# A mixture-of-experts decoder step on one core: scores of the next chunks between products, six outputs kept in PSUM, one bank each for scores and products

## The chip, the cores and the metric

One NeuronCore of a Trainium2 chip; the other cores are idle. The time is device microseconds of one execution of the whole program. TensorE is PE here, VectorE DVE, ScalarE ACT, GpSimd POOL, and SyncE, which issues most transfers, SP.

## The reference

One layer of a decoder trunk, for a prompt of 1024 tokens and for 8 sample sequences of one token each. The first half (normalisation, one projection, three mixers, output projection) is not touched by the change. The second half is PEER: each token picks, by two sets of 128 product keys, 16 experts in each of 8 heads out of 16,384, and each expert is one row of a table u and one row of a table v:

```
e_idx = i1 * N_KEYS + i2          # (n, 8 heads, 16) -> 128 experts per token
act = gelu(einsum('nd,nkd->nk', x, u_tab[e_idx]))
out = einsum('nk,nkd->nd', gate * act, v_tab[e_idx])
```

All in fp32; u_tab and v_tab hold 16,384 rows of 1024 numbers (4 KB a row, 64 MB a table).

## The kernel before

The 1024 prompt tokens are eight tiles of 128. Up to about 1720 us the kernel runs the first half and picks the experts. Then two ways of computing the experts run side by side.

**Gathered tiles** (prompt tiles 0, 2, 6 and 7, and the sample tile). For each of a token's 128 experts POOL issues an indirect transfer (L893, `gather_rows`) that brings one row of u per token, 128 rows of 4 KB, 512 KB in all, into one of five buffers `grow`; DVE multiplies and sums it (L901). After all 128, gelu and the gate, the same with v (L910, which adds into `acc`). L917 and L918 (`finish`) add the residual to a tile and SP stores it. The tiles come one after the other; the sample tile, eight rows of each table, is last, followed by a few small transfers and a reduction over its partial sums.

**Dense tiles** (prompt tiles 1, 3, 4 and 5, 512 tokens). Here all 16,384 experts are computed for all tokens, and a table of gates `g_d`, built before and zero where an expert wasn't picked, selects. There are 128 chunks of 128 experts. For each chunk `scores` loads 512 KB of u (L992), splits it into a high and a low part (`split`: cast on ACT, L968; difference on DVE, L969; named uh, ul), and multiplies by the tokens in 24 matmuls into one PSUM bank psS (L999: 8 pieces of the contraction, three products of high and low parts); ACT's gelu writes `a` (L1002), DVE multiplies by the gates gc (L1004; 2 MB of gates, for 8 chunks, are loaded by L989 into a single buffer), and `a` is split into ah and al. `load_v` loads 512 KB of v (L983) and splits it into vh, vl. Tables u and v come into RAW buffers `raw`, the split v into VB = 5.

Four chunks are a group. `products` multiplies a group's four `a` by its four v: eight outputs (4 tiles x 2 halves of 512 columns) of 12 matmuls each (L1015). RES of the outputs stay in PSUM over all groups (psK, the dictionary `keep`); the others go through the banks psO and are added by DVE to `acc` in SBUF (first group: copied, L1022; then L1024). PSUM has eight banks: four psK, two psS (SB) and two psO (OB). The loop runs one chunk ahead (SKEW = 1), so that PE works through the scores of four chunks and then through the eight products.

Both ways are written one after the other in the program; a scheduler that runs when the program is built puts each engine's instructions into one fixed order, by their dependences and estimated durations. So in the dense stretch each of DVE's and SP's lists alternates between the two. Each engine works through its list in order and waits where an operand isn't there. After the last group DVE multiplies the outputs by the gate g2 (L1043), adds the residual (L1044), and SP stores four tiles (L1045).

Of the kernel before, what the change touches and what calls it, by code (L numbers as in the profile page):

```python
# [16 lines left out]
ALU = mybir.AluOpType  # L17
# [10 lines left out]
GRP = 4  # L28
# [3 lines left out]
GST = 8  # L32
LK = 2
SJ = 4
RES = 4
RAW = 6
VB = 5
AB = 2
A4 = 3
SB = 2  # L40
OB = 2
SKEW = 1
GA = 3
GO = 1
GQ = 2
P = 128
# [13 lines left out]
def kernel(ctx: ExitStack, tc: tile.TileContext, I, O):  # L60
    nc = tc.nc
    V, A, G, T, S = nc.vector, nc.scalar, nc.gpsimd, nc.tensor, nc.sync
# [151 lines left out]
    def gate_row(which, t, alloc):  # L214

        m = alloc("grw")
        if t == NT:
            S.dma_start(m[:8], mods[which][0:8, :])
        else:
            S.dma_start(m, dram_ap(mods[which], 8 * D, [[0, P], [1, D]]))  # L220
        return m
# [10 lines left out]
    def product(st, t, xT, w):  # L232

        ps = st.ps("psz", "a")
        if t < NT:
            for c in range(8):
                T.matmul(ps, xT[:, c, :], w(c), start=(c == 0), stop=(c == 7))  # L237
            return ps
        for kk in range(2):
            for j in range(4):  # L240
                T.matmul(ps[32 * j:32 * j + 32, :], xT[:, 2 * j + kk, :], w(2 * j + kk), start=(kk == 0), stop=(kk == 1))
        part = st.a2("part")
        A.copy(part, ps)
        ps = st.ps("psz")
        T.matmul(ps[:8, :], sel[:, 0:8], part, start=True, stop=True)
        return ps
# [706 lines left out]
    def dense():  # L953
        n = ND * P
        parts = [(0, n)] if n <= 512 else [(0, n // 2), (n // 2, n)]
        outs = [(t, hf) for t in range(ND) for hf in range(2)]
        with tc.tile_pool(name="dn", bufs=2) as dn, tc.tile_pool(name="dps", bufs=1, space=PSUM) as dps:
            def ps_tile(name, bufs):
                return dps.tile([P, 512], F32, tag=name, name=name, bufs=bufs)

            def raw(name):
                return dn.tile([P, D], F32, tag="raw", name=name, bufs=RAW)

            def split(x, shape, key, bufs, eng):

                hi = dn.tile(shape, F32R, tag=key + "h", name=key + "h", bufs=bufs)
                lo = dn.tile(shape, F32R, tag=key + "l", name=key + "l", bufs=bufs)
                A.copy(hi, x)  # L968
                eng.tensor_tensor(lo, x, hi, op=ALU.subtract)  # L969
                return hi, lo  # L970

            xs_ = []
            for c in range(8):
                xr = raw("xr")[:, :n]
                S.dma_start(xr, xT_d[:, c, :])
                xs_.append(split(xr, [P, n], f"x{c}", 1, V))
            keep = {o: ps_tile(f"psK{o[0]}{o[1]}", 1) for o in outs[:RES]}
            acc = {o: dn.tile([P, 512], F32, name=f"acc{o[0]}{o[1]}", bufs=1) for o in outs[RES:]}
            gcs = {}

            def load_v(c):
                v = raw("v")
                S.dma_start(v, I["peer_v"][c * P:(c + 1) * P, :])  # L983
                return split(v, [P, D], "v", VB, V)

            def scores(c):
                if c % GST == 0:
                    gc = dn.tile([P, n // TB, GST, TB], F32, tag="gc", name="gc", bufs=1)
                    S.dma_start(gc, g_d[c // GST])  # L989
                    gcs[c // GST] = gc  # L990
                u = raw("u").rearrange("p (c k) -> p c k", c=8)
                S.dma_start(u, I["peer_uT"][c])  # L992
                us_ = split(u, [P, 8, P], "u", 2, V)
                a = dn.tile([P, n], F32, tag="a", name="a", bufs=AB)
                pss = [ps_tile("psS", SB) for _ in parts]
                for ps, (n0, n1) in zip(pss, parts):
                    for j in range(8):
                        for q, (x, y) in enumerate(((0, 0), (0, 1), (1, 0))):
                            T.matmul(ps[:, :n1 - n0], us_[x][:, j, :], xs_[j][y][:, n0:n1],  # L999
                                     start=(j == 0 and q == 0), stop=(j == 7 and q == 2))  # L1000
                for ps, (n0, n1) in zip(pss, parts):
                    A.activation(a[:, n0:n1], ps[:, :n1 - n0], AF.Gelu_apprx_tanh)  # L1002
                a3 = a.rearrange("p (b n) -> p b n", n=TB)
                V.tensor_tensor(a3, a3, gcs[c // GST][:, :, c % GST, :], op=ALU.mult)  # L1004
                return split(a, [P, n], "a", GRP + 1, V)

            def products(g, as_, vs_):
                first, last = g == 0, g == P // GRP - 1
                for o in outs:
                    t, hf = o  # L1010
                    ps = keep[o] if o in keep else ps_tile("psO", OB)
                    k = 0
                    for aa, vv in zip(as_, vs_):
                        for x, y in ((0, 0), (0, 1), (1, 0)):
                            T.matmul(ps, aa[x][:, t * P:(t + 1) * P], vv[y][:, hf * 512:(hf + 1) * 512],  # L1015
                                     start=(k == 0 and (first or o not in keep)),
                                     stop=(k == 3 * GRP - 1 and (last or o not in keep)))
                            k += 1
                    if o in keep:
                        continue  # L1020
                    if first:
                        V.tensor_copy(acc[o], ps)  # L1022
                    else:
                        V.tensor_tensor(acc[o], acc[o], ps, op=ALU.add)  # L1024

            ahead = [scores(c) for c in range(SKEW)]
            for g in range(P // GRP):
                as_ = list(ahead)
                vs_ = []
                for c in range(g * GRP, (g + 1) * GRP):  # L1030
                    if c >= g * GRP + SKEW:
                        as_.append(scores(c))
                    vs_.append(load_v(c))
                ahead = [scores(c) for c in range((g + 1) * GRP, (g + 1) * GRP + SKEW) if c < P]
                products(g, as_, vs_)
            g2 = gate_row("g2", DENSE[0], raw)
            for j, t in enumerate(DENSE):
                x1, tmp = raw("x1f"), raw("tmp")
                S.dma_start(x1, x1_d[t])
                for hf in range(2):  # L1040
                    sl = slice(hf * 512, (hf + 1) * 512)
                    src = keep[j, hf] if (j, hf) in keep else acc[j, hf]
                    V.tensor_tensor(tmp[:, sl], g2[:, sl], src, op=ALU.mult)  # L1043
                V.tensor_tensor(x1, x1, tmp, op=ALU.add)  # L1044
                S.dma_start(O["xp"][t * P:(t + 1) * P, :], x1)  # L1045
# [31 lines left out]
    for t in GROUPS[-1]:  # L1077
        if t in DENSE:
            now(select(t))
            now(gate_table(t))  # L1080
    fctx.close()
    dense()
    for t in GROUPS[-1]:
        if t not in DENSE:
# [91 lines left out]
```

## Time and profile before

| | us |
|---|---|
| median of 3 runs | 3323.45 (3322.58 to 3325.24) |
| profiled execution | 3327.76 |
| its span | 3326.0 |
| PE, DVE, ACT, POOL busy | 2795.2, 2543.4, 1201.9, 1394.1 |
| DMA | 952.56 MB, mean 286 GB/s |

The busy times are sums over stages with different limits. The change touches the last one alone, from about 1720 us to the end. A matmul's record shows 0.39 us or more, but the next starts earlier; how long a row of matmuls takes is read from the starts. The same holds on DVE and ACT, where a record reaches a little into the next.

### The profile page before, as it was taken

The page shows a single profiled execution, that of the slowest core. Times are in us where ns is not written, and L with a number is a line of the kernel's source. Part 1 is how long each engine was busy: PE and PEld are TensorE (multiplying, and loading weights), DVE is VectorE, ACT ScalarE, POOL GpSimd, SP SyncE. Part 2 cuts the span into 40 slices and gives each one's busy share as a digit, 9 for nine tenths or more (in the row PEclk, how much of TensorE's full clock was granted, in tenths as well). Part 3 has the DMA queues.
Part 4 walks back from the last instruction along what each step waited for, and adds up shares of the span by engine and source line. Part 5 has one row for each costly group of instructions (what it writes and reads, how often), then busy time and mean ns, then how long its engine had stood idle before and what let it go on. Part 6 is the DMA issues. An engine that isn't in the chain of part 4 may idle for free.

```text
span 3326.0 us, 35751 instructions
## 1 busy us (share of the span) xinstructions
PE 2795.2 (84%) x11152; PEld 1879.5 (57%) x11152; DVE 2543.4 (76%) x5342; ACT 1201.9 (36%) x2583; POOL 1394.1 (42%) x1046
## 2 busy tenths in 40 slices
PE   7999976868944888976759998988989988989997
PEld 2444353423630333554437777777777776777776
DVE  1324876896675777876799898788898888898896
ACT  2453474443630342664543222222222222222221
POOL 0000043414235532034323565466566656566563
PEclk8999997987955999987879999999999999999998
DMA  7556677947787987478887999899999999999996
GB/s 276 179 195 198 217 250 269 335 170 287 221 253 247 352 261 285 139 229 296 276 287 252 347 333 334 301 345 339 348 329 342 344 344 342 360 332 333 346 347 218
DMA packets 340157, 952.56 MB, mean 286 GB/s; under 512 B 35063, under 2 KB 117550, under 8 KB 337918
## 3 DMA queue, kind: packets, MB, share of 16 engines
q0 software_dynamic: 149760, 545.33, 46.6%
q1 hardware_dynamic: 190206, 404.95, 35.1%
q8 instruction: 88, 1.44, 0.2%
q14 instruction: 103, 0.84, 0.1%
HBM read 894.04 MB, written 60.85 MB: 287 GB/s over the span
## 4 chain that ended last, share of the span: by engine, by line
PE 27%; DMA 23%; issue 20%; POOL 14%; DVE 12%; ACT 3%; SPq 0%; POOLq 0%; DVEq 0%; ACTq 0%
POOL grow L893 14%; PE psz L237 10%; DMA grow<-in_peer_v,ge 8%; DMA g_d<-st 5%; PE psG L804 3%; DVE grow L901 3%; DMA grow<-in_peer_u,ge 2%; PE pst L162 2%; PE pso L622 2%; PE psS L999 2%; PE psO L1015 2%; PE lg L605 2%; PE psa L194 2%; DVE acc L910 1%; DMA w<-in_w_in 1%
## 5 line engine op out<-in xcount | busy, mean ns | idle before, releaser
L893 POOL DMA_INDIRECT grow<-in_peer_u,ge x520 | 685.2, 1318 | 1333.2 <-DVE grow L901 540.5
L893 POOL DMA_INDIRECT grow<-in_peer_v,ge x520 | 708.3, 1362 | 565.7 <-DVE acc L910 359.2
L910 DVE SCALAR_TENSOR_TENSOR acc<-grow,dot,acc 128x1024 f32<-128x1024 f32 x515 | 660.1, 1282 | 136.6 <-DMA grow<-in_peer_v,ge 129.5
L237 PE MATMUL psz<-w,hT 128*128 128x512 f32 x1408 | 682.7, 617 | 59.4 <-DMA w<-in_w_in 28.4
L901 DVE SCALAR_TENSOR_TENSOR grow<-grow,gx 128x1024 f32<-128x1024 f32 x520 | 625.8, 1219 | 133.5 <-DMA grow<-in_peer_u,ge 108.9
L237 PEld LDWEIGHTS psz<-w,hT 128*128 128x128 f32 x1408 | 253.2, 196 | 324.1 <-issue 223.0
L1015 PE MATMUL psO<-vh,ah 128*128 128x512 f32 x512 | 223.2, 436 | 120.8 <-DVE acc L1024 120.3
L804 PE MATMUL psG<-o,oh 128*128 128x128 f32 x1024 | 205.8, 339 | 121.0 <-ACT st L805 113.3
L968 ACT CAST vh<-v 128x1024 fp32r<-128x1024 f32 x128 | 125.2, 1048 | 492.5 <-PE psO L1015 491.1
L804 PEld LDWEIGHTS psG<-o,oh 128*128 128x128 f32 x1024 | 170.9, 232 | 208.7 <-ACT st L805 147.8
L796 DVE TENSOR_TENSOR oh<-iof,tr 128x1024 f32<-128x1024 f32 x128 | 156.5, 1224 | 134.2 <-PE psG L804 129.5
L968 ACT CAST ah<-a 128x512 fp32r<-128x512 f32 x128 | 79.6, 622 | 398.0 <-DVE a L1004 398.0
L968 ACT CAST uh<-u 128x1024 fp32r<-128x1024 f32 x128 | 135.1, 1055 | 236.6 <-PE psS L999 236.4
L1015 PE MATMUL psO<-vl,ah 128*128 128x512 f32 x512 | 216.9, 424 | 0.0
L1015 PE MATMUL psO<-vh,al 128*128 128x512 f32 x512 | 215.2, 420 | 0.0
L803 ACT ACTIVATE o<-oh,tr 128x128 f32<-128x128 f32 x512 | 185.5, 397 | 53.2 <-PE psG L804 44.0
L1015 PE MATMUL psK<-vh,al 128*128 128x512 f32 x512 | 199.9, 391 | 5.0 <-DVE al L969 5.0
L1015 PE MATMUL psK<-vh,ah 128*128 128x512 f32 x512 | 200.0, 391 | 2.3 <-ACT ah L968 2.3
L1015 PE MATMUL psK<-vl,ah 128*128 128x512 f32 x512 | 199.8, 390 | 0.0
L1015 PEld LDWEIGHTS psO<-vh,ah 128*128 128x128 f32 x512 | 107.2, 209 | 159.8 <-DVE acc L1024 136.3
L969 DVE TENSOR_TENSOR ul<-u,uh 128x1024 fp32r<-128x1024 f32 x128 | 156.1, 1220 | 5.5 <-ACT uh L968 5.5
L969 DVE TENSOR_TENSOR vl<-v,vh 128x1024 fp32r<-128x1024 f32 x128 | 150.6, 1219 | 0.5 <-ACT vh L968 0.4
(370 smaller groups left out, 5002.8 us busy)
## 6 DMA issues: line engine op xcount, KB each, us to landing
u<-in_peer_uT SPq DMA_DIRECT2D x128, 512.0 KB
v<-in_peer_v SPq DMA_DIRECT2D x128, 512.0 KB
w<-in_w_in SPq DMA_DIRECT2D x80, 512.0 KB
w<-in_wq SPq DMA_DIRECT2D x64, 512.0 KB
g_d<-st SPq DMA_DIRECT2D x32, 1024.0 KB
gc<-g_d SPq DMA_DIRECT2D x16, 2048.0 KB
w<-in_w_ada SPq DMA_DIRECT2D x48, 512.0 KB
w<-in_w_out SPq DMA_DIRECT2D x32, 512.0 KB
```

What stands on the lines that cost most here:

```text
L162: T.transpose(pv[:, c, :r], src[:, (c0 + c) * P:(c0 + c + 1) * P], ident[:r, :r])
L194: T.matmul(ps[32 * j:32 * j + 32, :], sc[:, 2 * j + kk, :], w(2 * j + kk), start=(kk == 0), stop=(kk == 1 and j > 0))
L237: T.matmul(ps, xT[:, c, :], w(c), start=(c == 0), stop=(c == 7))
L796: V.tensor_tensor(oh, iof[:, None, None, :].to_broadcast([P, 2, OHB, P]), tt[:, 0:2, b * TB + n0:b * TB + n0 + OHB, None].to_broadcast([P, ...
L803: A.activation(o1, oh[:, 0, n0 % OHB + q, :], AF.Copy, scale=tt[:, 2, n:n + 1])
L804: T.matmul(ps[:, q * P:(q + 1) * P], oh[:, 1, n0 % OHB + q, :], o1, start=True, stop=True)
L893: G.indirect_dma_start(out=rt, out_offset=None, in_=tab, in_offset=bass.IndirectOffsetOnAxis(ap=idx, axis=0))
L901: V.scalar_tensor_tensor(rt, rt, 1.0, x, op0=ALU.mult, op1=ALU.mult, accum_out=w[:, k:k + 1])
L910: V.scalar_tensor_tensor(acc, rt, w[:, k:k + 1], acc, op0=ALU.mult, op1=ALU.add)
L968: A.copy(hi, x)
L969: eng.tensor_tensor(lo, x, hi, op=ALU.subtract)
L1015: T.matmul(ps, aa[x][:, t * P:(t + 1) * P], vv[y][:, hf * 512:(hf + 1) * 512], start=(k == 0 and (first or o not in keep)), stop=(k == 3 * ...
```

## The change

- RES goes from 4 to 6: six outputs are kept in PSUM, and two, of tile 3, go through psO and `acc`. SB and OB go from 2 to 1, so the eight banks are six psK, one psS, one psO.
- RAW goes from 6 to 5, and the split `a` has 7 buffers in place of 5.
- SKEW falls away. `scores` of a whole group of four chunks runs ahead. In the loop, the scores of one chunk of the next group are followed by two of the eight products of this group, in the order of `turns`: outputs 0, 2, then 4, 6, then 1, 3, then 5, 7 of `outs`; those at the places 6 and 7 are the two that go through psO, so they are the fourth and the eighth product of a group. The four v of a group are loaded ahead of the scores of the next group.

Unchanged are the gathered tiles' code, the number of matmuls, all transfers and their sizes. Lines after the constants stand one or two lower: the casts are L967 and L968, loads L982, L988, L991, rows L900 and L909, finish L916 and L917, copies and additions L1020 and L1022. There were 128 copies and additions of outputs, now there are 64.

```diff
-RES = 4
-RAW = 6
+RES = 6
+RAW = 5
...
-SB = 2
-OB = 2
-SKEW = 1
+SB = 1
+OB = 1
...
-                return split(a, [P, n], "a", GRP + 1, V)
-
-            def products(g, as_, vs_):
+                return split(a, [P, n], "a", 2 * GRP - 1, V)
+
+            def product(g, o, as_, vs_):
                 first, last = g == 0, g == P // GRP - 1
-                for o in outs:
-                    t, hf = o
-                    ps = keep[o] if o in keep else ps_tile("psO", OB)
...
+                t, hf = o
+                ps = keep[o] if o in keep else ps_tile("psO", OB)
...
-            ahead = [scores(c) for c in range(SKEW)]
+            share = len(outs) // GRP
+            turns = sorted(outs, key=lambda o: (outs.index(o) % share, outs.index(o)))
+            ahead = [scores(c) for c in range(GRP)]
             for g in range(P // GRP):
-                as_ = list(ahead)
-                vs_ = []
-                for c in range(g * GRP, (g + 1) * GRP):
-                    if c >= g * GRP + SKEW:
-                        as_.append(scores(c))
-                    vs_.append(load_v(c))
-                ahead = [scores(c) for c in range((g + 1) * GRP, (g + 1) * GRP + SKEW) if c < P]
-                products(g, as_, vs_)
+                as_, ahead = ahead, []
+                vs_ = [load_v(c) for c in range(g * GRP, (g + 1) * GRP)]
+                for i in range(GRP):
+                    if g < P // GRP - 1:
+                        ahead.append(scores((g + 1) * GRP + i))
+                    for o in turns[i * share:(i + 1) * share]:
+                        product(g, o, as_, vs_)
```

Where the instructions stand now, at three places. First DVE's list near the end of a group, late in the last gathered tile, before. The rows `acc<-grow,dot,acc` are gathered rows, `acc_10713` to `acc_10716` the four outputs that are added in SBUF; a number behind x says how many stand in a row.

```order
L910 SCALAR_TENSOR_TENSOR acc<-grow,dot,acc 128x1024 x3
L1004 TENSOR_TENSOR a<-a,gc 128x512
L910 SCALAR_TENSOR_TENSOR acc<-grow,dot,acc 128x1024
L969 TENSOR_TENSOR al<-a,ah 128x512
L910 SCALAR_TENSOR_TENSOR acc<-grow,dot,acc 128x1024 x5
L1024 TENSOR_TENSOR acc_10713<-acc_10713,psO 128x512
L910 SCALAR_TENSOR_TENSOR acc<-grow,dot,acc 128x1024
L1024 TENSOR_TENSOR acc_10714<-acc_10714,psO 128x512
L910 SCALAR_TENSOR_TENSOR acc<-grow,dot,acc 128x1024 x2
L1024 TENSOR_TENSOR acc_10715<-acc_10715,psO 128x512
L910 SCALAR_TENSOR_TENSOR acc<-grow,dot,acc 128x1024
L969 TENSOR_TENSOR vl<-v,vh 128x1024
```

And now, from the end of one group (its last three vl) on, at about the same place of the program:

```order
L968 TENSOR_TENSOR vl<-v,vh 128x1024 x3
L909 SCALAR_TENSOR_TENSOR acc<-grow,dot,acc 128x1024 x2
L1003 TENSOR_TENSOR a<-a,gc 128x512
L968 TENSOR_TENSOR ul<-u,uh 128x1024
L968 TENSOR_TENSOR al<-a,ah 128x512
L968 TENSOR_TENSOR vl<-v,vh 128x1024
L909 SCALAR_TENSOR_TENSOR acc<-grow,dot,acc 128x1024 x6
L1003 TENSOR_TENSOR a<-a,gc 128x512
L968 TENSOR_TENSOR ul<-u,uh 128x1024
L968 TENSOR_TENSOR al<-a,ah 128x512
L909 SCALAR_TENSOR_TENSOR acc<-grow,dot,acc 128x1024
L1022 TENSOR_TENSOR acc_10715<-acc_10715,psO 128x512
```

Before, the run of rows and additions stood behind the group's scores; now up to seven rows stand between one chunk's steps and the next's, one addition comes after every second chunk, and behind the three vl of a group comes the vl of the next group's first v.

Second, SP's list of loads for one group, before (numbers are those of the tiles):

```order
L983 DMA v_18343<-in_peer_v 128x1024
L992 DMA u_18349<-in_peer_uT 128x1024
L983 DMA v_18387<-in_peer_v 128x1024
L992 DMA u_18393<-in_peer_uT 128x1024
L983 DMA v_18431<-in_peer_v 128x1024
L992 DMA u_18437<-in_peer_uT 128x1024
L983 DMA v_18475<-in_peer_v 128x1024
L992 DMA u_18483<-in_peer_uT 128x1024
```

and now:

```order
L982 DMA v_18073<-in_peer_v 128x1024
L982 DMA v_18079<-in_peer_v 128x1024
L982 DMA v_18085<-in_peer_v 128x1024
L982 DMA v_18091<-in_peer_v 128x1024
L991 DMA u_18097<-in_peer_uT 128x1024
L991 DMA u_18159<-in_peer_uT 128x1024
L991 DMA u_18223<-in_peer_uT 128x1024
L991 DMA u_18285<-in_peer_uT 128x1024
```

Where a u and a v alternated, a group's four v stand in a row ahead of four u.

Third, DVE's list around the finish of the last gathered tile (`grw` and `x1f` in its operands), before:

```order
L1004 TENSOR_TENSOR a<-a,gc 128x512
L969 TENSOR_TENSOR ul<-u,uh 128x1024
L969 TENSOR_TENSOR al<-a,ah 128x512
L910 SCALAR_TENSOR_TENSOR acc<-grow,dot,acc 128x1024 x5
L917 TENSOR_TENSOR acc<-acc,grw 128x1024
L918 TENSOR_TENSOR acc<-acc,x1f 128x1024
L1024 TENSOR_TENSOR acc_10713<-acc_10713,psO 128x512
L1024 TENSOR_TENSOR acc_10714<-acc_10714,psO 128x512
L1024 TENSOR_TENSOR acc_10715<-acc_10715,psO 128x512
L901 SCALAR_TENSOR_TENSOR grow,dot<-grow,gx 128x1024
L969 TENSOR_TENSOR vl<-v,vh 128x1024
```

and now:

```order
L1003 TENSOR_TENSOR a<-a,gc 128x512
L968 TENSOR_TENSOR ul<-u,uh 128x1024
L968 TENSOR_TENSOR al<-a,ah 128x512
L909 SCALAR_TENSOR_TENSOR acc<-grow,dot,acc 128x1024 x5
L916 TENSOR_TENSOR acc<-acc,grw 128x1024
L917 TENSOR_TENSOR acc<-acc,x1f 128x1024
L1003 TENSOR_TENSOR a<-a,gc 128x512
L968 TENSOR_TENSOR ul<-u,uh 128x1024
L968 TENSOR_TENSOR al<-a,ah 128x512
L968 TENSOR_TENSOR vl<-v,vh 128x1024
L1022 TENSOR_TENSOR acc_10716<-acc_10716,psO 128x512
```

Before, the finish stood behind ul of chunk 127 of 128 and a of chunk 126, and after it came the sample tile's rows and the last group's v; now it stands behind ul of chunk 121 and a of chunk 119, and three groups' vl come after it but for one.

## Rows read from the trace of the kernel before

**Rows 1.** One window of the stretch of dense and gathered work; columns in its first line.

```profile
core 0: us, PE busy (x) PEld busy (x) DVE busy (x) ACT busy (x) POOL busy (x), PEclk, DMA share, GB/s
1774.00:3257.00 1483.00, 1357.42 (x5737) 1107.00 (x5736) 1289.72 (x1528) 379.50 (x485) 890.18 (x646) 0.95 0.93 338
```

**Rows 2.** Instructions by line, VectorE, 1760 to 3260 us: the additions of outputs.

```profile
L1024 DVE TENSOR_TENSOR acc<-acc,psO 128x512 f32<-128x512 f32 x118 | 80.4, 682 | 3.9 <-PE psO L1015 3.9
```

**Rows 3.** Waits of VectorE, 1760 to 3260 us (total us, times, longest us).

```profile
DVE acc L910 <- DMA grow<-in_peer_v,ge: 86.6, 71, 5.4
DVE grow L901 <- DMA grow<-in_peer_u,ge: 66.9, 67, 5.6
```

**Rows 4.** Waits of TensorE, same stretch.

```profile
PE psO L1015 <- DVE acc L1024: 120.3, 33, 8.8
```

**Rows 5.** Waits of ScalarE, same stretch.

```profile
ACT vh L968 <- PE psO L1015: 474.2, 29, 22.4
```

**Rows 6.** Timeline of ScalarE: casts of v at four group boundaries (start, duration).

```profile
1774.31 3.90 ACT L968 CAST vh<-v 128x1024 fp32r<-128x1024 f32 x4
...
2822.17 3.90 ACT L968 CAST vh<-v 128x1024 fp32r<-128x1024 f32 x4 [16.66 <-PE psO L1015]
...
2868.83 3.90 ACT L968 CAST vh<-v 128x1024 fp32r<-128x1024 f32 x4 [18.94 <-PE psO L1015]
...
3261.93 2.95 ACT L968 CAST vh<-v 128x1024 fp32r<-128x1024 f32 x3 [16.89 <-PE psO L1015]
```

**Rows 7.** Timeline of TensorE: first and last of 37 matmuls in a row; the last matmul.

```profile
3247.68 0.39 PE L1015 MATMUL psK<-vl,ah 128*128 128x512 f32 x1
...
3255.84 0.39 PE L1015 MATMUL psO<-vl,ah 128*128 128x512 f32 x1
...
3310.91 0.39 PE L1015 MATMUL psO<-vh,al 128*128 128x512 f32 x1
```

**Rows 8.** Timeline of VectorE in the tail: last tile's finish, steps in a row, last addition.

```profile
3255.41 1.22 DVE L918 TENSOR_TENSOR acc<-acc,x1f 128x1024 f32<-128x1024 f32 x1
...
3270.30 1.22 DVE L969 TENSOR_TENSOR vl<-v,vh 128x1024 fp32r<-128x1024 f32 x1
3271.44 0.68 DVE L1024 TENSOR_TENSOR acc<-acc,psO 128x512 f32<-128x512 f32 x1
3272.04 2.36 DVE L969 TENSOR_TENSOR vl<-v,vh 128x1024 fp32r<-128x1024 f32 x2
...
3275.45 1.22 DVE L901 SCALAR_TENSOR_TENSOR grow<-grow,gx 128x1024 f32<-128x1024 f32 x1
...
3276.60 1.22 DVE L901 SCALAR_TENSOR_TENSOR grow<-grow,gx 128x1024 f32<-128x1024 f32 x1
...
3311.34 0.69 DVE L1024 TENSOR_TENSOR acc<-acc,psO 128x512 f32<-128x512 f32 x1 [1.30 <-PE psO L1015]
...
3312.78 1.23 DVE L1044 TENSOR_TENSOR x1f<-x1f,tmp 128x1024 f32<-128x1024 f32 x1
```

**Rows 9.** Chain of waits in the tail: three transfers of 512 KB (start, us).

```profile
3256.66 5.92 DMA out_xp<-acc
3262.59 6.46 DMA gx<-h_d
...
3277.79 7.92 DMA grow<-in_peer_u,ge
```

**Rows 10.** Windows of 10 us in the stretch (columns as in rows 1).

```profile
2400.00:2410.00 10.00, 10.00 (x45) 8.28 (x45) 4.21 (x4) 0.00 (x0) 3.54 (x3) 1.00 1.00 414
2410.00:2420.00 10.00, 4.49 (x20) 3.38 (x18) 9.42 (x9) 0.62 (x1) 6.21 (x6) 0.88 0.84 286
2720.00:2730.00 10.00, 10.00 (x45) 8.26 (x44) 10.00 (x15) 5.45 (x6) 4.88 (x4) 1.00 0.89 313
```

**Rows 11.** Instructions by line, ScalarE, 1760 to 3260 us: cast of v, gelu.

```profile
L968 ACT CAST vh<-v 128x1024 fp32r<-128x1024 f32 x120 | 117.0, 1048 | 474.2 <-PE psO L1015 474.2
...
L1002 ACT ACTIVATE a<-psS 128x512 f32<-128x512 f32 x120 | 70.7, 589 | 0.0
```

More of the change, by code (lines that the diff above doesn't have):

```diff
@@ L1004, in scores @@
                 V.tensor_tensor(a3, a3, gcs[c // GST][:, :, c % GST, :], op=ALU.mult)
-                return split(a, [P, n], "a", GRP + 1, V)
-            def products(g, as_, vs_):
+                return split(a, [P, n], "a", 2 * GRP - 1, V)
+            def product(g, o, as_, vs_):
                 first, last = g == 0, g == P // GRP - 1
-                for o in outs:
-                    t, hf = o
-                    ps = keep[o] if o in keep else ps_tile("psO", OB)
[L1012 to L1024, printed above, removed]
@@ new lines, in product @@
+                ps = keep[o] if o in keep else ps_tile("psO", OB)
+                k = 0
+                for aa, vv in zip(as_, vs_):
+                    for x, y in ((0, 0), (0, 1), (1, 0)):
+                        T.matmul(ps, aa[x][:, t * P:(t + 1) * P], vv[y][:, hf * 512:(hf + 1) * 512],
+                                 start=(k == 0 and (first or o not in keep)),
+                                 stop=(k == 3 * GRP - 1 and (last or o not in keep)))
+                        k += 1
+                if o in keep:
+                    return
@@ new lines, in product @@
+                if first:
+                    V.tensor_copy(acc[o], ps)
+                else:
+                    V.tensor_tensor(acc[o], acc[o], ps, op=ALU.add)
+            share = len(outs) // GRP
+            turns = sorted(outs, key=lambda o: (outs.index(o) % share, outs.index(o)))
+            ahead = [scores(c) for c in range(GRP)]
+            for g in range(P // GRP):
+                as_, ahead = ahead, []
[5 more added lines that the diff above has]
+                        product(g, o, as_, vs_)
```

## The prediction

> **What bounds the kernel now.** I read the stretch in which dense work and gathered rows run side by side first, since nothing before it changes. From 1774 to 3257 us [rows 1] PE is busy 1357 of 1483 us, VectorE (DVE) 1290 and the DMA engines 93% of the time: three resources near their ends. Which one holds the others shows in the waits. DVE waits almost only for gathered rows, 86.6 + 66.9 = 153.5 us [rows 3], and hardly for PE. PE, in turn, stands 120.3 us for DVE's additions of finished outputs [rows 4], and ScalarE (ACT) stands before the casts of v for PE's last product [rows 5]: followers. So DVE, working through its list in order, sets the pace, and what it lacks are rows. PE's own need is smaller: 37 product matmuls start over 8.16 us [rows 7], 8.16 / 36 = 0.2267 us each, 192 in a group of four chunks, 43.5 us; the casts of v, four in a row, mark the groups, 30 of them from 1774.31 to 3261.93 [rows 6], 49.6 us on average, and 46.7 for one of the shorter (2822.17 to 2868.83). The end is a tail: the last gathered tile is done at 3255.41 + 1.22 = 3256.6 [rows 8], the span ends at 3326.0, 69.4 us later, with the sample rows and the last products in it.
>
> The rows lack evenness: in the order of before they come in runs of some 15 behind the scores, 2 or 3 to a chunk ahead of them. Over 10 us the DMA share goes from 0.84 to 1.00, and from 286 to 414 GB/s; in a slice in which DVE works without a gap the share is only 0.89 [rows 10]. DMA has little left, but has some.
>
> **The change part by part.** All against the profiled execution, 3327.76 us, which is 4.3 above the median.
>
> *Additions.* Two outputs instead of four go through the bank pair and an addition. An addition takes 3272.04 - 3271.44 = 0.60 us of DVE from start to start [rows 8]; the line stands 118 times in the stretch [rows 2]. Before the last gathered tile is done I count 120 of before (30 groups) and 57 now: 63 x 0.60 = **-37.8**.
>
> *Chunks that move behind the gather.* A chunk costs DVE ul and vl, 1.14 each (vl at 3270.30, next at 3271.44), and a and al, as large as an addition, 0.60 each [rows 8]. The order of the change has gathered rows in all the room that the additions leave, so that the last tile's finish stands behind ul of chunk 121, not 127, a of chunk 119, not 126, and vl of 117, not 124: 6 x 1.14 + 7 x 1.14 + 7 x 1.20 = **-23.2** ahead of that finish. These are not saved, they are paid in the tail.
>
> *Row waits.* Evenly placed rows (about 7, then 2 + 5, between the steps of one chunk and the next) should cut the 153.5 us; fuller DMA queues should lengthen each wait. I keep the sum of waits. The check is the DMA share: the stretch holds 0.93 x 1483 = 1379 us of DMA work; 6 u and 7 v loads fall out, 13 x 0.524 MB at 338 GB/s and share 0.93 = 18.7, so 1361. Done in 57 us less, that is a share of 1361 / 1426 = 0.954. Bounds: at 0.93 (nothing evened) the stretch shortens by 20 only; at 1.00 [rows 10] by 122.
>
> *RAW 6 to 5.* A group's four v now load ahead of its u's, and one is always late: the next group's first v takes the buffer that this group's second v frees (its vl, at the boundary), and DVE reaches that v's own vl after two vl, two rows, a, ul and perhaps al: 2.28 + 2.30 + 0.60 + 1.14 = 6.3 us, or 6.9 with al [rows 8], in about half the groups; 8.7 in the others. A transfer of that size took 6.46 (gx) in the tail, a row 7.92 [rows 9], and the cast on ACT 1.05 [rows 11]: 7.5 against 6.6, a stop of 0.9 on DVE in 14 groups, 13 us. Nothing waits behind it on SP but the same group's other loads; on ACT the uh casts and gelu stand behind vh. Rows go on landing during the stop, so I let two thirds come out of the row waits: **+4** (bounds 0, and 38 below). The 2 MB gate load every second group waits for the last reader of its only buffer as before: 0.
>
> *Scores between products, one bank each, a held in 7 buffers.* The bank of scores is used again after two products, 24 x 0.2267 = 5.4 us, and ACT's gelu takes 0.59 [rows 11]; the output bank again after 84 matmuls, 19 us, against an addition of 0.68. Taken at 0, hidden under the products; what it costs if that cover goes is the third rival. The Trainium skill ("Perfetto Trace Analysis", section "Matmuls") says that independent matmul groups should rotate through different PSUM banks, so that the emptying of one overlaps the next; here the other kind of group lies between, and the rows give room. The 120 us that PE stood for additions go; PE was not the bound, so they bring nothing themselves. At a boundary PE has one block of scores (5.4 us) to cover the v casts, not four, and will stand there.
>
> *Tail.* When the last gathered tile is done, a of chunk 120 is next on DVE. If PE is ahead it has the two products after that chunk's scores, 8 blocks of scores and 24 products left: (24 + 192 + 288) = 504 matmuls, 114 us. If DVE holds it, PE has run one block further and waits for the v casts: 456 matmuls, 103 us, plus 6.4 us of DVE until those are done, 110. I take 111. After the last matmul come an addition, two halves and the output: before, 3310.91 [rows 7] to 3312.78 + 1.23 [rows 8], and 5.92 for a store [rows 9], 9 us. So 120 instead of 69.4: **+50.5**. The sample rows, which ended the kernel before, are now over some 40 us earlier.
>
> Sum: -37.8 - 23.2 + 4 + 50.5 = -6.5, so 3321 beside the profiled 3327.76, and **3317** as a median. The likeliest case's own range comes from the DMA share: at 0.94 the stretch is 1447 long (36 shorter, 3338), at 0.965 1410 (73 shorter, 3301). A measurement of this kernel tells 0.2%, 6.6 us, from no change.
>
> **Rivals.**
> *The rows were short only because they were bunched* (faster). For it: share 1.00 in some slices, and groups of 46.7 beside the mean of 49.6. Against it: 200-us means hardly move. At a share of 0.975 the stretch takes 1396, 87 less: -87 + 50.5 = -37, **3286**.
> *The late v takes the place of the additions* (slower). Place: DVE's vl of the next group's first v, just behind a boundary. Price: with a landing like the longest in the tail, 7.92 + 1.05 - 6.6 = 2.4 us in 14 groups and 0.3 in 14 others, 38 us, and not won back because DMA idles too while five row buffers stand full; 34 more than in my sum, **3351**. It decides from the point at which load and cast exceed the 6.6 us. For it: the queues are 93% full. Against it: before, v's casts never waited on their loads; [rows 5] name PE alone, though there the buffers were free 20 or more DVE steps ahead.
> *One bank each makes PE the bound* (slower, the mechanism of the page named above). If ACT comes to gelu only behind the next uh cast, each block of scores stops PE 1.05 + 0.59 us, each addition 0.68: 4 x 1.64 + 2 x 0.68 = 7.9 a group, 51.4 in place of 49.6; 29 groups cost 8 more, the tail 20, with its 50.5: **3402**. Against it: the 5.4 us of products between.
> That the change doesn't do what it says is out by the order of instructions: the products do alternate, and 64 additions are gone.
>
> **How the numbers follow.** Forecast 0.47, evened rows 0.20, late v 0.30, PE the bound 0.03. Of the forecast's 0.47, half (0.23) lies below 3316.8, 0.15 within 6.6 us of the median, 0.09 above. With evened rows faster is 0.43; the late v gives 0.02 to no change and 0.28 to slower, and with the third rival slower is 0.40; no change 0.17. Range: down to a DMA share of 0.98 (1388 us, -95 + 50.5, 3279) and a little below, 3275, up past the late v with longer landings at the three boundaries of the tail too, 3372. Left out are the top of the late v, the third rival and a share of 1.00 (3252), together some 0.15.
>
> **What would show it.** Right: PE's waits for additions gone, 64 additions in all, the last finish some 57 us earlier (near 3200), and from there 120 us to the end with PE at 0.2267 a matmul; the DMA share near 0.954 until then; some stops of DVE or ACT before the cast of a first v, about 1 us. Wrong: a share that stays at 0.93 (the late v, or rows that were never bunched), a share over 0.97 (evened rows), PE waiting for gelu, or a tail shorter than 110 us, which would make my count of what is left in it the faulty step.

## The result, and the profile after

The changed kernel takes 3380.94 us (median of 4 runs, 3374.01 to 3383.29) against 3323.76 before (one execution more than in the table above): a ratio of 1.0167, 95% interval 1.0146 to 1.0189. It is 57 us slower, where 6 us less was forecast, and lies above the range.

The profiled execution has a span of 3381.2 us, 55.2 more than before. Three moments divide it: TensorE's first matmul of scores, the finish of the last gathered tile, the end. Ahead of the first nothing was changed, but it moves by some us from one execution to another, so everything below is counted from it. The rows of the first moment, before and after, from the timeline of TensorE:

```profile
1722.57 0.76 PE L999 MATMUL psS<-x0h,uh 128*128 128x512 f32 x1 [30.79 <-ACT uh L968]
```

```profile
1714.55 0.76 PE L998 MATMUL psS<-x0h,uh 128*128 128x512 f32 x1 [30.88 <-ACT uh L967]
```

The finish of after, on VectorE (DVE), at 3251.68 + 1.23 = 3252.9 (it answers to [rows 8]):

```profile
3251.68 1.23 DVE L917 TENSOR_TENSOR acc<-acc,x1f 128x1024 f32<-128x1024 f32 x1
```

So the stretch from the first scores to the last finish takes 1538.4 us (before 3256.6 - 1722.6 = 1534.1), and the tail from there to the end 128.3 (before 69.4). With the start 8.0 earlier: +4.3 + 58.9 - 8.0 = 55.2. The stretch was to be 57 shorter, the tail 50.5 longer.

One window over the stretch, before and after (columns as in [rows 1]):

```profile
1722.57:3256.63 1534.06, 1407.98 (x5945) 1147.88 (x5946) 1340.31 (x1682) 405.30 (x515) 894.79 (x650) 0.95 0.92 333
```

```profile
1714.55:3252.91 1538.36, 1372.93 (x5683) 1101.24 (x5684) 1283.18 (x1593) 377.68 (x491) 857.61 (x650) 0.93 0.91 326
```

DVE's work fell by 1340.3 - 1283.2 = 57.1 us, nearly the 61 of the forecast. Its idle time grew by 61.4, from 193.8 to 255.2. Its waits in the stretch (total us, times, longest) follow. For before, these are the ones beside the rows of [rows 3] that are compared below:

```profile
DVE grow L901 <- DMA gx<-h_d: 16.0, 2, 8.4
DVE a L1004 <- DMA gc<-g_d: 6.2, 1, 6.2
DVE acc L1024 <- PE psO L1015: 2.6, 7, 0.5
DVE a L1004 <- ACT a L1002: 0.7, 3, 0.3
DVE al L969 <- ACT ah L968: 0.7, 1, 0.7
DVE vl L969 <- ACT vh L968: 0.4, 2, 0.3
```

and for after, all of more than 3 us:

```profile
DVE grow L900 <- DMA grow<-in_peer_u,ge: 72.2, 64, 3.4
DVE acc L909 <- DMA grow<-in_peer_v,ge: 68.7, 69, 3.3
DVE vl L968 <- ACT vh L967: 49.2, 19, 4.8
DVE grow L900 <- DMA gx<-h_d: 20.9, 2, 11.0
DVE al L968 <- ACT ah L967: 12.6, 7, 2.7
DVE a L1003 <- DMA gc<-g_d: 12.1, 9, 2.7
DVE a L1003 <- ACT a L1001: 7.4, 8, 3.3
```

Rows cost 140.9 (before 153.5). New are 49.2 at vl, the low part of v, and beside it 12.6 at al and 7.4 at gelu's result: ScalarE (ACT) stood before the cast of a v that had not landed, and the casts and gelu that stand behind it in ACT's list came late. ACT's own wait, answering to [rows 5], and TensorE's (PE), answering to [rows 4]:

```profile
ACT vh L967 <- DMA v<-in_peer_v: 191.3, 30, 15.0
```

```profile
PE psK L1013 <- ACT vh L967: 80.7, 21, 7.1
PE psK L1013 <- DVE vl L968: 65.1, 36, 11.1
...
PE psS L998 <- ACT a L1001: 18.4, 11, 2.9
```

PE's 120.3 us for additions are gone; in their place stand 145.8 for the high and low parts of v at the group boundaries (127.9 of it stays in late_v_gone below, so most of it belongs to the new order and not to the late v). Before a block of scores PE waited 18.4 for gelu to empty the single bank.

One boundary shows how a v comes late. SyncE's (SP) queue, then ACT, then DVE, from their timelines:

```profile
2833.81 0.33 SPq L988 DMA_DIRECT2D gc<-g_d  x1
2834.97 0.33 SPq L991 DMA_DIRECT2D u<-in_peer_uT  x1
2837.82 10.38 SPq L982 DMA_DIRECT2D v<-in_peer_v  x4
```

```profile
2846.71 0.62 ACT L967 CAST ah<-a 128x512 fp32r<-128x512 f32 x1 [7.95 <-DVE a L1003]
2851.13 1.05 ACT L967 CAST vh<-v 128x1024 fp32r<-128x1024 f32 x1 [3.79 <-DMA v<-in_peer_v]
```

```profile
2836.58 1.22 DVE L968 TENSOR_TENSOR vl<-v,vh 128x1024 fp32r<-128x1024 f32 x1
...
2847.73 0.68 DVE L968 TENSOR_TENSOR al<-a,ah 128x512 fp32r<-128x512 f32 x1
2852.21 1.23 DVE L968 TENSOR_TENSOR vl<-v,vh 128x1024 fp32r<-128x1024 f32 x1 [3.79 <-ACT vh L967]
```

The load of the next group's first v is issued at 2837.82, as soon as the second v's vl is done; DVE reaches its vl at 2848.4, and the cast starts at 2851.13: 13.3 us after the issue, and DVE lost 3.8. A 2 MB gate load and a u had been issued 4.0 and 2.9 us before it.

Only every second boundary has a gate load. At the next one the same load found none, and the cast began 6.4 us after the issue:

```profile
2893.35 10.16 SPq L982 DMA_DIRECT2D v<-in_peer_v  x4
2899.72 1.05 ACT L967 CAST vh<-v 128x1024 fp32r<-128x1024 f32 x1 [6.88 <-DMA v<-in_peer_v]
```

So it is over the whole stretch: at the 14 boundaries with a gate load issued 4 to 5 us ahead, the cast began 9.1 to 13.5 us after the issue (median 11.7), at 14 without one 4.5 to 7.3 (median 6.5). Of DVE's 49.2 us at vl, 34.1 fell at the first kind and 15.2 at the second. (No run took the gate load away with the late v in place; a u stands a few us ahead at both kinds.)

### The profile page after: what moved, and what is told of

Its sections match the earlier page's. It is cut to its first block, busy times and chain, and to the rows that moved or that the text cites. A ratio compares the mean times of both kernels' runs of the same rounds, so it can differ in the third digit from the quotient of the medians.

```text
span 3381.2 us, 35692 instructions
## 1 busy us (share of the span) xinstructions
PE 2813.6 (83%) x11152; PEld 1880.0 (56%) x11152; DVE 2510.7 (74%) x5278; ACT 1193.1 (35%) x2583; POOL 1363.5 (40%) x1046
## 4 chain that ended last, share of the span: by engine, by line
issue 24%; DMA 20%; POOL 14%; PE 12%; DVE 7%; ACT 2%; POOLq 0%; SPq 0%; DVEq 0%; ACTq 0%
POOL grow L892 14%; DMA grow<-in_peer_v,ge 9%; DMA g_d<-st 4%; PE psz L236 3%; PE psG L803 2%; DVE acc L909 1%; PE pso L621 1%; DVE grow L900 1%; PE lg L604 1%; DMA vc<-in_cache_v 1%; DMA grow<-in_peer_u,ge 1%; PE pst L161 1%; DMA gc<-g_d 1%; PE psS L998 1%; PE psK L1013 1%
## 5 line engine op out<-in xcount | busy, mean ns | idle before, releaser
L892 POOL DMA_INDIRECT grow<-in_peer_u,ge x520 | 675.7, 1299 | 1342.1 <-DVE grow L900 542.3
L892 POOL DMA_INDIRECT grow<-in_peer_v,ge x520 | 687.1, 1321 | 597.5 <-DVE acc L909 386.2
L909 DVE SCALAR_TENSOR_TENSOR acc<-grow,dot,acc 128x1024 f32<-128x1024 f32 x515 | 660.1, 1282 | 118.2 <-DMA grow<-in_peer_v,ge 110.2
L900 DVE SCALAR_TENSOR_TENSOR grow<-grow,gx 128x1024 f32<-128x1024 f32 x520 | 624.7, 1219 | 142.3 <-DMA grow<-in_peer_u,ge 111.7
L1013 PE MATMUL psK<-vh,ah 128*128 128x512 f32 x768 | 322.5, 420 | 86.7 <-ACT vh L967 86.7
L1013 PE MATMUL psK<-vl,ah 128*128 128x512 f32 x768 | 328.5, 428 | 70.1 <-DVE vl L968 69.1
L967 ACT CAST ah<-a 128x512 fp32r<-128x512 f32 x128 | 79.5, 621 | 855.4 <-DVE a L1003 852.8
L1013 PE MATMUL psK<-vh,al 128*128 128x512 f32 x768 | 317.4, 413 | 0.0
L1013 PEld LDWEIGHTS psK<-vh,ah 128*128 128x128 f32 x768 | 156.7, 204 | 130.7 <-ACT vh L967 96.5
L1013 PEld LDWEIGHTS psK<-vl,ah 128*128 128x128 f32 x768 | 155.4, 202 | 132.0 <-DVE vl L968 102.6
L967 ACT CAST vh<-v 128x1024 fp32r<-128x1024 f32 x128 | 127.7, 1044 | 196.2 <-DMA v<-in_peer_v 196.2
L968 DVE TENSOR_TENSOR vl<-v,vh 128x1024 fp32r<-128x1024 f32 x128 | 152.4, 1220 | 52.2 <-ACT vh L967 52.2
L967 ACT CAST uh<-u 128x1024 fp32r<-128x1024 f32 x128 | 134.3, 1049 | 155.5 <-PE psS L998 155.5
L1013 PEld LDWEIGHTS psK<-vh,al 128*128 128x128 f32 x768 | 157.5, 205 | 29.3
L968 DVE TENSOR_TENSOR ul<-u,uh 128x1024 fp32r<-128x1024 f32 x128 | 156.0, 1219 | 9.4 <-ACT uh L967 9.4
L804 ACT COPY st<-psG 128x512 f32<-128x512 f32 x128 | 74.7, 584 | 153.4 <-DMA g_d<-st 113.8
```

The lines of the kernel that those rows point to most:

```text
L804: A.copy(st[:, :, n0:n0 + 4], ps.rearrange("p (n c) -> p c n", n=4))
L892: G.indirect_dma_start(out=rt, out_offset=None, in_=tab, in_offset=bass.IndirectOffsetOnAxis(ap=idx, axis=0))
L900: V.scalar_tensor_tensor(rt, rt, 1.0, x, op0=ALU.mult, op1=ALU.mult, accum_out=w[:, k:k + 1])
L909: V.scalar_tensor_tensor(acc, rt, w[:, k:k + 1], acc, op0=ALU.mult, op1=ALU.add)
```

## The experiments

All runs below are compared with the kernel of before on the same chip. The table is worked out from their profiles: dense start to last finish (stretch), finish to end (tail), DVE's busy time in the stretch, and its waits for gathered rows there. The expectations name the finish as it stands in the profile, with the start, which moves by some us, in it.

| run | ratio to before (95%) | stretch | tail | DVE busy | waits for rows |
|---|---|---|---|---|---|
| before | 1 | 1534 | 69 | 1340 | 153.5 |
| after | 1.0167 (1.0146 to 1.0189) | 1538 | 128 | 1283 | 140.9 |
| late_v_gone | 1.0080 (1.0053 to 1.0106) | 1507 | 126 | 1282 | 172.5 |
| old_loop_raw5 | 1.0211 (1.0179 to 1.0242) | 1613 | 68 | 1343 | 145.6 |
| old_loop_six_kept | 1.0240 (1.0211 to 1.0269) | 1545 | 143 | 1283 | 200.1 |
| old_loop_five_kept | 1.0207 (1.0159 to 1.0256) | 1576 | 84 | 1328 | 184.7 |
| new_loop_four_kept | 1.0060 (1.0036 to 1.0083) | 1546 | 76 | 1344 | 147.7 |
| new_loop_five_kept | 1.0055 (1.0031 to 1.0079) | 1525 | 95 | 1309 | 162.9 |
| old_loop_raw8 | 1.0013 (0.9989 to 1.0036) | 1537 | 74 | 1338 | 162.9 |
| no_gate_loads | 0.9897 (0.9859 to 0.9936) | 1458 | 118 | 1280 | 140.7 |
| late_v_gone_grow4 | 1.0458 (1.0417 to 1.0500) | 1627 | 103 | 1292 | 286.1 |
| old_loop_seven_rows | 0.9761 (0.9730 to 0.9793) | 1448 | 69 | 1334 | 57.6 |
| new_loop_six_rows | 0.9943 (0.9923 to 0.9964) | 1453 | 127 | 1278 | 118.8 |

**late_v_gone.** Against after:

```diff
-RAW = 5
-VB = 5
+RAW = 7
+VB = 4
```

> The changed kernel with RAW 7 and VB 4 (same bytes of SBUF): every v has its own raw buffer long before the group boundary (37 or more VectorE steps between the release of its buffer and its use, instead of 6 to 10), and all four v are cast at the boundary. Theory 1 (late v: the first v of the next group, loaded only at the boundary, stops ScalarE and VectorE): ScalarE's waits for v's transfers fall from 187 us to under 20, VectorE's for the casts of v from 49 to under 10, the last gathered tile is done near 3200 us instead of 3253, the time is 3325 to 3340. Theory 2 (the transfers as a whole bound the stretch: what is not waited for at v is waited for at the rows): the finish stays at 3240 or later, the waits for rows grow by 30 us or more from 141, the time is 3365 or more. In both the tail from the finish to the end stays 118 to 130 us.

Measured: 3354.24 us, ratio 1.0080; the profiled execution, with a span of 3338.8, was the fastest, 13.5 us under the median. DVE's waits in its stretch:

```profile
DVE acc L909 <- DMA grow<-in_peer_v,ge: 94.3, 86, 3.0
DVE grow L900 <- DMA grow<-in_peer_u,ge: 78.2, 71, 2.6
DVE a L1003 <- DMA gc<-g_d: 25.3, 13, 3.9
```

ACT's waits for v's transfers and DVE's for v's casts are gone, and so are those at al and gelu: 68 us of waits. The stretch got 31 shorter (by the ratios, 1.0167 and 1.0080, the gain is 29 us). The other half came back as waits for rows (+31.6) and for gates (+13.2, to 25.3). The time lies between the two forecasts, and both theories hold in part: the late v costs about 30 us, and what then holds DVE are rows.

**old_loop_raw5.** Against before, `RAW = 6` to `RAW = 5` alone.

> The kernel of before with RAW 5 instead of 6, nothing else. Its list of instructions then has a late v too (6 VectorE steps between release and use in each group). Theory 1: 25 to 50 us slower than before (3350 to 3375), ScalarE waiting for v's transfers 100 us or more. Theory 2: within 10 us of before, since the same bytes move.

Measured: 3401.69 us, 1.0211. DVE's waits in its stretch:

```profile
DVE acc L910 <- DMA grow<-in_peer_v,ge: 84.4, 70, 6.1
DVE vl L969 <- ACT vh L968: 80.9, 33, 4.6
DVE grow L901 <- DMA grow<-in_peer_u,ge: 61.2, 48, 6.0
```

80.9 us at vl where there were 0.4, and the stretch is 78.6 longer, more than theory 1 had it. Here no gate load stands just ahead of the late v, and its cast began 4.6 to 8.6 us after the issue (median 7.3); but DVE reached its vl 5.4 us after it (median), and stopped at nearly every boundary. One raw buffer less, with not one byte more to move, costs more than the whole change did: theory 2 alone is out.

**old_loop_six_kept** and **old_loop_five_kept.** Against before:

```diff
-RES = 4
-SB = 2
-OB = 2
+RES = 6
+SB = 1
+OB = 1
```

and

```diff
-RES = 4
-OB = 2
+RES = 5
+OB = 1
```

> The loop, the order of loads and RAW 6 of before, with six outputs kept and one bank each for scores and products: the saved additions and the banks alone. The finish of the last gathered tile stands behind ul of chunk 119 in the order. Theory 1 (only the late v spoils the gain): the finish near 3195, then about 125 us of dense work left, 3315 to 3330, about as before. Theory 2: finish at 3235 or later, 3360 or more. If one bank for the scores stops TensorE (four blocks of scores follow each other here), it shows as waits of psS for gelu of 1 to 2 us for each chunk, 120 to 240 us in all.

> The loop of before with five outputs kept, two banks for scores, one for products, RAW 6: 96 copies and additions instead of 128; the finish of the last tile stands behind ul of chunk 126, so the tail is as long as before. Theory 1: 32 x 0.60 = 19 us less on VectorE, little given back: 3300 to 3312. Theory 2: 3318 to 3328, no change. If one bank for three added outputs in a row stops TensorE, its waits for additions grow from 120 us to 150 or more, without effect on VectorE.

Measured: 3409.75 us, 1.0240, and 3393.41 us, 1.0207. Six kept lies within the open bounds of theory 2 (finish at 3267.6), five kept outside both theories; neither names what held these runs. PE's wait for additions in the stretch, with six kept, then with five (before 120.3, [rows 4]):

```profile
PE psO L1015 <- DVE acc L1024: 190.1, 28, 11.0
```

```profile
PE psO L1015 <- DVE acc L1024: 165.4, 28, 10.8
```

and DVE's waits, with six kept, and with five for the products alone:

```profile
DVE acc L910 <- DMA grow<-in_peer_v,ge: 111.4, 79, 5.6
DVE grow L901 <- DMA grow<-in_peer_u,ge: 88.7, 67, 6.6
DVE acc L1024 <- PE psO L1015: 21.9, 22, 1.5
```

```profile
DVE acc L1024 <- PE psO L1015: 26.2, 23, 3.1
```

In the old loop the added outputs stand close together, and with one bank PE and DVE wait for one another: DVE for the product (21.9 and 26.2 us, before 2.6), PE for the addition. With six kept the rest is the tail, 143 us: 57 us of work less in the stretch only moved rows ahead of dense work. Why the waits for rows grow too (by 46.6 and 31.2) was not tried by itself. The single bank of scores did not stop PE: of the 120 to 240 us expected, 1.8 were there. But the four blocks of scores do not follow each other, as was expected: the order built for this run puts seven product matmuls between two blocks (read in PE's timeline from 2400 to 2500 us), so the run changes more than the banks.

**new_loop_four_kept** and **new_loop_five_kept.** The new loop without a late v, with more additions. Against after:

```diff
-RES = 6
-RAW = 5
-VB = 5
-SB = 1
-OB = 1
+RES = 4
+RAW = 6
+VB = 4
+SB = 2
+OB = 2
```

and the same with RES 5, SB 1.

> The new loop without a late v (VB 4, RAW 6) and with the PSUM of before: four outputs kept, two banks each, 128 copies and additions. In the order the last gathered tile's finish stands behind ul of chunk 128, not 121 or 122, so little dense work is left behind it. Tail theory (the saved additions were handed to rows, which moved the gather ahead of the dense work, and the dense work that was left ran alone at the end): the finish near 3250 to 3265, from there 65 to 80 us to the end, in all 3315 to 3340. Loop theory (the new loop itself loses, by TensorE's stops for v casts at each group boundary): the finish at 3275 or later, 3345 or more.

> The new loop without a late v (VB 4, RAW 6), five outputs kept, one bank for scores, two for products, 96 copies and additions; the finish stands behind ul of chunk 124. Tail theory: between late_v_gone and new_loop_four_kept, finish near 3230 to 3240, then 90 to 105 us, 3325 to 3345. Loop theory: 3345 or more, no better than late_v_gone.

Measured: 3350.71 us, 1.0060, and 3342.58 us, 1.0055. By the bounds that were written down, four kept falls to the loop theory and five kept to the tail theory. The tail goes as the tail theory has it, 76 and 95 us, with the place of the finish in the order: behind ul of chunk 128, 124, and 122 for late_v_gone (126 us). But the stretch takes it back: with the additions of before it is 12 us longer than in the old loop. DVE's waits in new_loop_four_kept:

```profile
DVE a L1003 <- DMA gc<-g_d: 16.8, 12, 3.2
```

The gate waits, 6.2 before, are 16.8. From the last reader of one gate table to DVE's arrival at the first reader of the next 15.4 us lie before (median of 14), 10.0 in new_loop_four_kept and 10.6 in after, and where DVE waited the table was read 10.1 to 13.0 us after the issue of its load. These waits are 11 of the 12 us more in the stretch in size; that they are its cause was not tried by itself. So the loop itself loses some 19 us by the profiles, and both theories explain a part.

**no_gate_loads** (late_v_gone with `if c == 0:` for the gate load, and `gcs[0]`).

> The run late_v_gone with the gate table loaded once instead of 16 times: 15 transfers of 2 MB, 31 MB of about 500 in the stretch, are left out, so chunks from the ninth on are weighted by the gates of the first eight. Transfer theory (DMA at 0.93 holds the stretch): 31 MB at 340 GB/s are 92 us, the last finish 60 us or more earlier than in late_v_gone, and the waits for rows fall below 120 us from 175. Latency theory (rows wait for their own round trip through five buffers and the queues are not the limit): only the 28 us of waits for gates go, the finish is 20 to 35 us earlier.

Measured: 3300.71 us, 0.9897. Its stretch is 49 shorter than that of late_v_gone: 25 of gate waits are gone and 32 of waits for rows, while some small waits grew.

```profile
DVE acc L909 <- DMA grow<-in_peer_v,ge: 78.5, 77, 2.3
DVE grow L900 <- DMA grow<-in_peer_u,ge: 62.2, 53, 3.2
```

```profile
1724.46:3182.33 1457.87, 1363.69 (x5688) 1096.22 (x5688) 1280.38 (x1594) 381.00 (x492) 885.32 (x650) 0.95 0.91 324
```

The finish is 30.5 earlier, as the latency theory had it; but the dense part began 18.7 later, and counted from there the shortening, and the fall of the row waits, lie between the two. Undecided. What it does show: with 6% fewer bytes the DMA share is 0.91, as in the stretch of after, at 324 GB/s.

**old_loop_raw8** (before with RAW 8, VB 4).

> The kernel of before with RAW 8 and VB 4 (same bytes of SBUF): before already casts a group's four v in a row at the boundary, so the fifth split buffer brings little, and u and v can be fetched further ahead. If loads are late in the kernel of before too: 10 to 30 us faster. If not (its v casts waited for no load): within 8 us of before.

Measured: 3330.04 us, 1.0013, no change. The loads of before were early enough, and with RAW 8 the fifth split buffer of v isn't needed there. (The step from VB 5 to 4 was not run alone.)

**late_v_gone_grow4** (late_v_gone with `bufs=4` for the row buffers `grow` and RAW 8).

> The run late_v_gone with four row buffers instead of five, and the freed 4 KB as an eighth raw buffer. Tail: the order has the last finish behind ul of chunk 124 instead of 122, so from the finish to the end 90 to 105 us instead of 126 (new_loop_five_kept, also 124, took 95). What holds the rows: if it is their round trip through the buffers (issue 1.3, landing 6.3, VectorE's step 1.2, about 9 us for each buffer), four buffers give a row each 2.25 us at best against 2.3 needed, and VectorE's waits for rows grow from 172 us to 230 or more, 3375 or more in all. If it is the transfers as a whole, the waits stay between 150 and 190, and the time is 3325 to 3350.

Measured: 3484.85 us, 1.0458. DVE's waits:

```profile
DVE acc L909 <- DMA grow<-in_peer_v,ge: 170.8, 136, 3.6
DVE grow L900 <- DMA grow<-in_peer_u,ge: 115.3, 99, 3.1
```

286.1 us for rows in place of 172.5, and 120 us more of stretch, as the round-trip theory has it: the rows are held by their way through the buffers. The tail, 103, is where the order put it.

**old_loop_seven_rows** and **new_loop_six_rows.** Against before (VB 5 to 4 pays for it):

```diff
-VB = 5
+VB = 4
...
-    def gather_rows(tab, idx):
-        rt = grow("grow")
+    more = {}
+
+    def gather_rows(tab, idx, k, t):
+        if t in (6, 7) and k % 7 in (1, 3):
+            rt = more["rows"].tile([P, D], F32, tag="grow2", name="grow", bufs=2)
+        else:
+            rt = grow("grow")
...
     fctx.close()
+    more["rows"] = ctx.enter_context(tc.tile_pool(name="gat2", bufs=2))
     dense()
```

with `k` and `t` handed on by `experts`; and against after the same with one buffer (`k % 6 == 1`), VB 4, RAW 6.

> The kernel of before with VB 4 and, from the freed 8 KB, two more row buffers for the gathered tiles 6 and 7 (512 of the stretch's 650 rows). The order is that of before (finish behind ul of chunk 127). Round-trip theory (rows wait for their way through five buffers): VectorE's waits for rows fall from 153 us to 60 to 100, the finish comes 50 to 90 us earlier after the start of the dense work than 1534 us, the tail stays about 70, in all 3240 to 3285. Transfer theory (queues at 0.92 are full): the waits stay above 135, the time within 10 us of before.

> The new loop without a late v (VB 4, RAW 6; six kept, one bank each) and one more row buffer, six, for tiles 6 and 7. The finish stands behind ul of chunk 121. Round-trip theory: against late_v_gone the waits for rows fall from 172 us to 100 to 140 and the stretch from 1507 to 1470 or less; the tail is TensorE's and stays 124 to 132: in all 3290 to 3320. Transfer theory: the stretch 1500 to 1515, 3335 to 3360.

Measured: 3246.85 us, 0.9761, and 3308.77 us, 0.9943. DVE's waits and the window, old_loop_seven_rows:

```profile
DVE acc L915 <- DMA grow<-in_peer_v,ge: 36.9, 37, 5.3
DVE a L1009 <- DMA gc<-g_d: 26.1, 9, 9.0
DVE grow L906 <- DMA grow<-in_peer_u,ge: 20.7, 23, 4.1
```

```profile
1721.89:3170.35 1448.46, 1375.64 (x5929) 1126.65 (x5930) 1333.71 (x1680) 404.51 (x514) 903.25 (x650) 0.98 0.95 353
```

The waits for rows fall from 153.5 to 57.6, the stretch by 86, at the same tail; the DMA share rises to 0.95 and the rate to 353 GB/s. All this is what the round-trip theory forecast, or a little more. The transfer theory, by which the waits stay above 135, is out. The new loop gains too: with one buffer its stretch is 54 us shorter than that of late_v_gone, and it keeps its tail of 127. The first of the two is 2.4% faster than before and the best version that was run.

## Why the prediction was wrong, point by point

*What bounds it.* That DVE sets the pace and lacks rows held: rows stay DVE's largest wait in every run, and the time follows them when row buffers are taken away or added. That the DMA share says how much room is left did not hold. I read 0.93 as nearly full and wrote the bounds as shares. Over the stretches of after, no_gate_loads and late_v_gone it stood at 0.91 at three rates, 326, 324 and 333 GB/s; with two more row buffers in the old loop it was 0.95, with one less in the new 0.87. In these runs it went up and down with the number of row buffers. What I should have weighed stands in the profile of before: POOL waits for DVE to free one of five buffers, and a row takes 6.5 us (median) from its issue to landing.

```profile
POOL grow L893 <- DVE acc L910: 247.6, 157, 6.1
POOL grow L893 <- DVE grow L901: 226.1, 104, 40.4
```

An estimate from these rows: 1.3 us for the issue on POOL, 6.5 to landing and 1.2 on DVE make 9 us, so five buffers give a row every 1.8 us at best, and the stretch's 650 rows in 1534 us ask for one every 2.4 on the average, for more where they come in runs. The Trainium skill ("Perfetto Trace Analysis", section "Optimization Strategy") names this case: the same gap over and over on the engine that should be busy can mean too few buffers for the next tile. The trace agrees, 153.5 us of such gaps before, 57.6 with seven buffers.

*Additions and moved chunks*, -37.8 - 23.2 = -61: measured -57.1 of DVE's busy time. Right. (By the trace of before the finish stands behind a and vl of chunk 125, not 126 and 124; the sum stays at -23.2.)

*Row waits*, kept: 140.9 for 153.5, near the truth in after, but by luck: DVE's stops at vl let rows land. With the late v gone they rose to 172.5, 19 more than before. Freed DVE time runs into the row buffers' round trip, so only a part of a saving on DVE shows here, and evened rows won 12.6 at most. This term, taken as kept, is the second that was wrong: without the late v the stretch is 27 shorter than before, where -61 was forecast for DVE's work.

*RAW 6 to 5*: **the step that failed.** The place was right (the next group's first v, loaded at the boundary); the size of the stop was not. I took 7.5 us for load and cast at every boundary against 6.6 until DVE arrives: 0.9 in 14 groups, 13 us, and +4 in the sum. Measured: 48.8 more at vl, 11.9 at al, 6.7 at gelu, 67 in all. Two things were left out. The gate load, for which I wrote 0, stands on SP just ahead of the late v at every second boundary, and there the load alone took 9.1 to 13.5 us, not 6.46: 34.1 of the 49.2 us at vl. At the others load and cast took about what I had priced, and 15.2 fell there. And that other casts and gelu stand behind vh on ACT was written down, and priced at nothing: DVE's waits for them grew by 19. late_v_gone gives 31 us of stretch back, so this step is about half of what the stretch missed by (+4.3 for -57); rows and gates are the rest. My rival had the net price nearly right, 38, but from a landing of 7.92 us in all groups; it ended at 3351, as it kept the forecast's other terms.

*Gates*, priced at 0: 5.9 more in after, 19 more once the late v was gone. Too small: the new order leaves 10.6 us in place of 15.4 between a table's last reader and the next one's first. What the gate load does to the late v behind it was not seen at all.

*Banks and a.* In the stretch PE waited 18.4 us for gelu (5.0 with the late v gone) and never for an addition, so 0 was nearly right. The Trainium skill's rule ("Perfetto Trace Analysis", section "Matmuls"), to rotate independent groups through different banks, costs little to break here, where other groups lie between; in the old loop PE's waits for additions went from 120.3 us with two output banks to 190.1 and 165.4 with one.

*Tail*, +50.5: measured 58.9, because PE also waited there, for v's casts and once for gelu:

```profile
PE psK L1013 <- ACT vh L967: 6.1, 2, 5.9
PE psK L1013 <- DVE vl L968: 4.0, 4, 2.3
PE psS L998 <- ACT a L1001: 1.2, 1, 1.2
```

111 + 9 + 11.3 is 131, 3 over what was measured. 8.2 of the 11.3 fell at 3308.98 and 3312.05: the sample tile's rows, which I took to be over early and without effect, stood in DVE's list ahead of what PE needed. The count of what is left when the gather ends was right. With it late_v_gone still ends later than before: 57 more in the tail, 27 less in the stretch.

## What to carry to other kernels

Where one engine's list interleaves two jobs, work saved on it goes to the job that the order lets run ahead, and the other runs alone at the end: count what is left at the moment the first one ends. Before counting a saving on an engine that waits for a ring of buffers, price the ring (buffers against round trip): here one raw buffer less cost the old loop 79 us of stretch, one row buffer more gave the new one 54, and the saved additions were 38. And a transfer that is issued at a group boundary is priced with the transfers issued just ahead of it there: here it took nearly twice as long behind a gate load as without one.

## What the runs showed of the hardware

In after, a 512 KB load was usable 9.1 to 13.5 us from its issue at the 14 boundaries with a 2 MB load issued 4 to 5 us before it, and 4.5 to 7.3 us at the 14 without; 5.9 to 7.9 us were read in the tail of before. The DMA share over the stretch stood at 0.91 with 324 GB/s (no_gate_loads) and with 333 (late_v_gone), and two more row buffers raised it to 0.95 with 353, so a share of 0.91 did not say how much more could be moved.
